# RWKV-7 triangular inverse spread over 128 partitions, with HGRN's first level by copies, fills on GpSimd and the copies into M moved ahead

## The chip, the cores and the metric

The kernel runs on one core of one Trainium2 chip. The metric is the device time of one execution, in microseconds (us). The engines are TensorE (PE, with its weight loads as PEld), VectorE (DVE), ScalarE (ACT), GpSimd (POOL) and SyncE (SP, which issues most DMAs here). Each engine runs its own instructions in order.

## The reference

One decoder layer on x of shape (1, 2048, 1024), in float32. Cut to what matters:

```
h = RMSNorm(x)
[hgrn2 columns | rwkv7 columns] = h @ W_in
HGRN2, 4 heads of 128:  S_t = diag(f_t) S_{t-1} + k_t v_t^T ;  o_t = S_t^T q_t     (k = 1 - f, chunks of 64)
RWKV-7, 8 heads of 64:  S_t = S_{t-1} diag(w_t) + (S_{t-1} a_t) b_t^T + v_t k_t^T ;  y_t = S_t r_t
x = x + concat(o_hgrn2, o_rwkv7) @ W_out
x = x + ConvFFN(RMSNorm(x))     (up-projection, causal convolution of width 3, SiLU gate, down-projection)
out = RMSNorm(x)
```

The kernel computes both recurrences by chunks. In RWKV-7 the product (S a) b^T couples the steps of a chunk, so that each chunk of 64 steps and each head needs the inverse of a unit lower triangular 64x64 matrix. In HGRN2 the decay between two steps of a chunk is a product of the f of the steps between them, and the kernel builds it in levels of a binary tree: at level l a chunk is cut into pairs of stretches of 2^l steps.

## The kernel before, in words

Phase 1 (about half of the time) makes the input projection, both mixers and the output projection of three of four blocks of 512 steps (nb = 0 to 3); phase 2 makes the last output block and the ConvFFN. A float32 product is three products of fp32r halves: each operand is split into a high half (a cast on ACT, L243 for weights, L236 for activations) and a low half (a subtraction on DVE, L244 and L237), and `mm3` issues hi x hi, hi x lo and lo x hi (L259 to L261).

**The order of the work.** Phase 1 interleaves three Python generators: `dense()` issues projections, one column job of 24 matmuls at a time (weights `wraw`, L546), and output blocks (`out_block`, activations `oraw`, L375, weights `woraw`, L382, six matmuls per k); `rw_stream` runs eight times `rw_super` (two per block); `hg_stream` runs 16 times `hg_unit` (four per block). In the loop at the end of `phase1` the two mixer generators step once each, then `fill` lets dense work go on for a credit of TICK = 2000. A list scheduler then fixes the order of each engine's instructions. A consumer waits for its producers by semaphores; a buffer with n copies comes free when its last reader is done. SP's one queue issues nearly all loads, and so weight loads stand behind whatever was put ahead of them. Only the last block's outputs are stored by GpSimd's queue (`last_dma`). Weight buffers (`wraw`, `woraw`, `oraw` share them) hold four raw tiles and four pairs of split halves.

**`rw_super`**, one half of a block (two heads pairs u, 64 triangular blocks of 32x32):
- the front makes KB, AR and the masked products M on PE (L683 to L698);
- eight DMAs take the 64 diagonal 32x32 blocks of M to DRAM (`Ed`, L711), one brings them back as E with one block on each of 64 partitions (L713);
- KBT, RHS and UV are filled by copies on ACT;
- Ti is set to the identity by two fills on DVE (L757, L758), and 31 column steps make the inverse on 64 partitions: a product E column x Ti row (L764) and an addition into the rows below (L766), with j + 1 columns and 31 - j rows at step j; a yield every four steps;
- Ti goes to DRAM (L770), a transposed copy TiT (DVE, L771) too (L772); eight DMAs bring TiT back into TTs (L779), four bring Ti back into TZ (L782);
- z (L790) and z2 (L803) combine the two diagonal 32x32 inverses of a 64x64 block with its off-diagonal block, with copies into TZ and TTs on ACT (through the helper `act`, L117);
- qus (L816) applies the inverse, one PSUM tile for each u; its result goes by seven ACT copies into M (three) and UV (four), in the order M(u0), UV, UV, M, UV, M, UV; L841 reads M, and L844, L847 (DVE) make AR; L857, L864 follow;
- the recurrence over the chunks (L875 on PE, L877 on DVE), then output and norm (L885, L893, L905) and the store to `oT` (L908). L841's tile takes the PSUM slot of the first qus tile.

**`hg_unit`**, one head of one block: k = 1 - f (L916); Sf is set to one (DVE, L927); `scaled(l)` for levels 0 to 6 makes X from q x Pf (L934) and k x Sf (L935) and updates Sf (L937) and Pf (L939); `level` multiplies X by itself on PE (L955), `take` picks the results into A (L961); two ACT copies A into Af; L990 and L991 scale k and q; L997 to L1023 finish the unit, L1029 stores to `oT`.

At level 0 a stretch has one step, Sf is still one and Pf is still f.

Of the kernel before, what the change touches and what calls it, by code (L numbers as in the profile page):

```python
# [7 lines left out]
F32 = mybir.dt.float32  # L8
# [3 lines left out]
AF = mybir.ActivationFunctionType  # L12
# [6 lines left out]
P = 128  # L19
# [42 lines left out]
def tile_layer(ctx, tc, consts, x, norm1_w, w_in, hg_lb_logits, hg_norm_w, rw_shift_mu, rw_w0, rw_w2,  # L62
# [3 lines left out]
    nc = tc.nc  # L66
    V, S, TE = nc.vector, nc.scalar, nc.tensor
    dma = nc.sync.dma_start

    cp = ctx.enter_context(tc.tile_pool(name="cp", bufs=1, reuse_waits="tile"))  # L70
    dp = ctx.enter_context(tc.tile_pool(name="dp", bufs=1, space=DRAM))
# [37 lines left out]
    def act(out_, in_, func, **kw):  # L109

        want = tables.get(func)
        if want is not None and want != tab["now"]:
            pre = S.preload_act_table_set(want)
            for u_ in tab["uses"]:
                tc.add_manual_dep(pre.ins, u_.ins.name, NOSYNC, reason="table order")
            tab.update(now=want, pre=pre, uses=[])
        i_ = S.activation(out_, in_, func, **kw)  # L117
        if want is not None:
            tc.add_manual_dep(i_.ins, tab["pre"].ins.name, NOSYNC, reason="table order")
            tab["uses"].append(i_)  # L120
        return i_
# [13 lines left out]
    with tc.tile_pool(name="vp", bufs=1, reuse_waits="tile") as vp, tc.tile_pool(name="ps0", bufs=1, space=PSUM, reuse_waits="tile") as pools["ps"]:  # L135
        rows = vp.tile([P, P], F32, name="rows")
        V.memset(rows, 0.0)
        n = 0
# [124 lines left out]
    def phase1(c1):  # L263
# [3 lines left out]
        rp = c1.enter_context(tc.tile_pool(name="rp", bufs=1, reuse_waits="tile"))  # L267
# [10 lines left out]
        TTs = hp.tile([P, 16, 64], F32, name="TTs")  # L278
# [326 lines left out]
        er0 = lambda e: 64 if e == 0 else 0  # L605

        def quads():

            return [(b, h, e, u) for b in range(4) for h in range(2) for e in range(2) for u in U]

        def col0(u, e):

            return er0(e) if u == 0 else 64 - er0(e)
# [3 lines left out]
        U = range(2)  # L617

        def rw_super(nb, s_):

            tl = stage[("tl", nb)]
            r, k, v = (stage.pop(("rkv", nb, s_, w)) for w in range(3))
# [3 lines left out]
            def tile_(tag, shape, name):  # L626
                return rp.tile([P] + shape, F32, tag=tag, name=name)

            def bank2():
                return ps.tile([P, 2, BLK], F32, tag="rw", name="rw", bufs=2)  # L630

            ai = tile_("KBT", [2, 2, BLK], "ai")
            a, iW = ai[:, 0], ai[:, 1]
# [9 lines left out]
            c, km, sq = mk_[:, 0], mk_[:, 1], mk_[:, 2]  # L643
# [43 lines left out]
            M = tile_("M", [2, 2, 4, 2, P], "M")  # L687
            for j in range(2):
                for u in U:
                    s1 = bank2()  # L690
                    for i in range(4):
                        b, e = 2 * j + i // 2, i % 2
# [9 lines left out]

            E = rp.tile([P, 32, 32], F32, tag="E", name="E")
            Ed = dp.tile([64, 32, 32], F32, tag="Ed", name="Ed", bufs=2)
            Td = dp.tile([2, 64, 32, 32], F32, tag="Td", name="Td", bufs=2)
            for u in U:
                for e in range(2):
                    for q in range(2):
                        r0 = er0(e) + 32 * q
                        m0 = u * 32 + (e * 2 + q) * 8  # L710
                        dma(Ed[m0:m0 + 8].rearrange("m s t -> s m t"),  # L711
                            M[r0:r0 + 32, u, e, :, :, 32 * q:32 * q + 32].rearrange("p b h t -> p (b h) t"))
            dma(E[0:64], Ed)  # L713

            KBT = tile_("KBT", [2, 8, P], "KBT")
            for u in U:
# [7 lines left out]
            UV = tile_("UV", [8, 2, P], "UV")  # L724
# [18 lines left out]
            for b, h, e, u in quads():  # L743
                kr, c0, sl = 64 - er0(e), col0(u, e), (b * 2 + h) * 64
# [5 lines left out]
            for e in range(2):  # L750
                r0, c0 = er0(e), col0(1, e)
                act(RHS[r0:r0 + 64, 4:8, :, 64:128], lvv[c0:c0 + 64, 1], AF.Copy)
            yield

            n = 64
            Ti = rp.tile([P, 32, 32], F32, tag="Ti", name="Ti")
            V.memset(Ti[0:n], 0.0)  # L757
            V.memset(Ti[0:n].rearrange("m a b -> m (a b)")[:, 0:1024:33], 1.0)  # L758
            yield
            for j in range(31):  # L760
                nr, ncol = 31 - j, j + 1
                tmp = rp.tile([P, 272], F32, tag="etmp", name="etmp")
                tv = tmp[0:n, 0:nr * ncol].rearrange("m (a b) -> m a b", b=ncol)
                V.tensor_mul(tv, E[0:n, j, j + 1:32].unsqueeze(2).broadcast_to([n, nr, ncol]),  # L764
                             Ti[0:n, j, 0:ncol].unsqueeze(1).broadcast_to([n, nr, ncol]))
                V.tensor_add(Ti[0:n, j + 1:32, 0:ncol], Ti[0:n, j + 1:32, 0:ncol], tv)  # L766
                if j % 4 == 3:
                    yield
            TiT = rp.tile([P, 32, 32], F32, tag="E", name="TiT")
            dma(Td[0], Ti[0:n])  # L770
            V.tensor_copy(TiT[0:n], Ti[0:n].rearrange("m a b -> m b a"))  # L771
            dma(Td[1], TiT[0:n])  # L772
            TZ = tile_("XH", [2, 2, 4, 2, 32], "TZ")
            for u in U:
                for e in range(2):
                    r0 = er0(e)
                    for q in range(2):
                        m0 = u * 32 + (e * 2 + q) * 8
                        dma(TTs[r0 + 32 * q:r0 + 32 * q + 32, 8 * u:8 * u + 8, 32 * q:32 * q + 32],  # L779
                            Td[1, m0:m0 + 8].rearrange("m s t -> s m t"))  # L780
                    m0 = u * 32 + e * 16
                    dma(TZ[r0:r0 + 32, 0, u].rearrange("p b h t -> p (b h) t"),  # L782
                        Td[0, m0:m0 + 8].rearrange("m s t -> s m t"))
            for _ in range(2):
                yield
            z = bank2()
            for b, h, e, u in quads():
                r0 = er0(e)
                c0, sl = r0 + 32 - 32 * u, u * 256 + (b * 2 + h) * 32
                TE.matmul(z[c0:c0 + 32, 0, sl:sl + 32], M[r0:r0 + 32, u, e, b, h, 32:64],  # L790
                          TZ[r0:r0 + 32, 0, u, b, h, :], start=True, stop=True, tile_position=(r0, c0))
            for u in U:
                for e in range(2):
                    r1 = er0(e) + 32
                    c0 = r1 - 32 * u
                    act(TZ[r1:r1 + 32, 1, u].rearrange("p b h t -> p (b h t)"),
                        z[c0:c0 + 32, 0, u * 256:u * 256 + 256], AF.Copy)
            yield
            z2 = bank2()
            for b, h, e, u in quads():  # L800
                r0 = er0(e)
                c0, sl = r0 + 32 * u, u * 256 + (b * 2 + h) * 32
# [3 lines left out]
            for u in U:  # L806
                for e in range(2):
                    r0 = er0(e)
                    c0 = r0 + 32 * u
# [3 lines left out]
            qus = [bank2() for _ in U]  # L813
            for b, h, e, u in quads():
                r0, c0, sl = er0(e), col0(u, e), ((b % 2) * 2 + h) * P
                TE.matmul(qus[u][c0:c0 + 64, b // 2, sl:sl + P], TTs[r0:r0 + 64, u * 8 + b * 2 + h, :],  # L816
                          RHS[r0:r0 + 64, 4 * u + b, h, :], start=True, stop=True, tile_position=(r0, c0))
            for u in U:
                quv = qus[u].rearrange("p j (b h t) -> p (j b) h t", h=2, t=P)
                bs = slice(4 * u, 4 * u + 4)  # L820
                if u == 0:
                    act(M[:, u, 0, :, :, 0:64], quv[:, :, :, 0:64], AF.Copy)
                for e in range(2):
                    r0, c0 = er0(e), col0(u, e)
                    if u == 1:
                        act(M[r0:r0 + 64, u, 0, :, :, 0:64], quv[c0:c0 + 64, :, :, 0:64], AF.Copy)
                    act(UV[r0:r0 + 64, bs, e, :].rearrange("p b (h t) -> p b h t", t=64),
                        quv[c0:c0 + 64, :, :, 64:128], AF.Copy)
            yield
            for u in U:  # L830
                Q, G = M[:, u, 0, :, :, 0:64], M[:, u, 1, :, :, 0:64]
# [21 lines left out]
            for u in U:  # L853
                for ch in range(8):
                    b, e = ch // 2, ch % 2
# [4 lines left out]
            for u in U:  # L860
                for ch in range(8):
                    b, e = ch // 2, ch % 2
# [6 lines left out]
            for ch in range(8):  # L869
                b, e = ch // 2, ch % 2  # L870
# [42 lines left out]
        def hg_unit(nb, j):  # L913
            q, f, v, gg = (stage.pop((n_, nb, j)) for n_ in "qfvg")
            k = rp.tile([P, BLK], F32, tag="hk", name="hk")
# [8 lines left out]
            A = rp.tile([P, 4, 64], F32, tag="hA", name="A")  # L924
            Pf = f
            Sf = rp.tile([P, BLK], F32, tag="Sf", name="Sf")
            V.memset(Sf, 1.0)  # L927

            def scaled(l):

                m = 1 << l
                X = rp.tile([P, BLK], F32, tag="hX", name="hX", bufs=3)
                vw = lambda t_: t_.rearrange("p (n e m) -> p n e m", e=2, m=m)
                V.tensor_mul(vw(X)[:, :, 1, :], vw(q)[:, :, 1, :], vw(Pf)[:, :, 1, :])  # L934
                V.tensor_mul(vw(X)[:, :, 0, :], vw(k)[:, :, 0, :], vw(Sf)[:, :, 0, :])  # L935
                n_ = BLK // (2 * m)
                V.tensor_mul(vw(Sf)[:, :, 0, :], vw(Sf)[:, :, 0, :],  # L937
                             vw(Pf)[:, :, 1, m - 1:m].broadcast_to([P, n_, m]))
                V.tensor_mul(vw(Pf)[:, :, 1, :], vw(Pf)[:, :, 1, :],  # L939
                             vw(Pf)[:, :, 0, m - 1:m].broadcast_to([P, n_, m]))  # L940
                return X
# [24 lines left out]
            for l in range(3):  # L966
                Xs.append(scaled(l))
                yield
# [9 lines left out]
            for l in range(3, 6):  # L978
                Xs.append(scaled(l))
                yield  # L980
# [8 lines left out]
            X = scaled(6)  # L989
# [101 lines left out]
    with ExitStack() as c2:  # L1091
# [35 lines left out]
        with tc.tile_pool(name="op", bufs=1, reuse_waits="tile") as op_:  # L1127
# [4 lines left out]
            b = NBLK - 1  # L1132
# [34 lines left out]
            for dh in range(2):  # L1167
                accs = [pst("wacc") for _ in range(4)]
                for n, k in enumerate((0, 1, 4, 5, 2, 3, 6, 7)):
# [10 lines left out]
                    if dh == 1 and 2 <= n:  # L1180
                        for j in range(2):
                            q = 2 * (n - 2) + j
# [198 lines left out]
    with tc.tile_pool(name="dn", bufs=1, reuse_waits="tile") as dn:  # L1381
# [59 lines left out]
        for s_ in range(3, N):  # L1441
            g, p, kk = steps[s_]
# [53 lines left out]
```

## Time and profile before

| what | value |
|---|---|
| time, median of three runs | 2762.55 us (2758.13 to 2766.44) |
| the profiled execution: its own time, its span | 2766.94 us, 2765.2 us |
| mean granted TensorE clock | 0.983 |
| ACT busy | 1426.2 us |
| issues of E, TZ, TTs on SP | 8, 32, 64 |

A row of the profile that begins with a line and an engine is a group of equal instructions: operation, output<-input by the program's names, partitions x elements, count | busy us in total, mean ns of one | idle time of the engine just before them, and what ended it. A row of waits reads: engine, what waited, <- what released it: us in total, times, longest. A row of the timeline begins with start and length in us, and ends with the idle time before it in brackets. "pj", "rw", "hg" and "wacc" are PSUM tiles of dense work, `rw_super`, `hg_unit` and the last output block.

### The profile page before, as it was taken

How to read it: one execution, taken by the hardware profiler on the slowest of the kernel's cores; microseconds unless marked ns; L12 is line 12 of the kernel's file. 1: busy time of each engine (PE TensorE's matmuls, PEld its weight loads, DVE VectorE, ACT ScalarE, POOL GpSimd, SP SyncE). 2: the span in 40 equal slices, each digit the busy share in tenths (PEclk: the TensorE clock that was granted, in tenths of full speed). 3: DMA queues.
4: the chain of work that ended last, by engine and by line, in shares of the span. 5: the costliest groups of instructions: out<-in, count | busy, mean ns of one | idle time of the engine just before them, and what ended most of it. 6: DMA issues, size and time to landing. Idle time of an engine off the chain costs nothing. (4 is left out here: it accounts for less than half of the span.)

```text
span 2765.2 us, 47846 instructions
## 1 busy us (share of the span) xinstructions
PE 2650.8 (96%) x18059; PEld 2107.8 (76%) x18059; DVE 2067.1 (75%) x3877; ACT 1426.2 (52%) x2304; POOL 11.1 (0%) x24
## 2 busy tenths in 40 slices
PE   8999999989999999999889999998999999999998
PEld 6877777766776777767667888786888888877887
DVE  5868787685686766768658889988997877677656
ACT  5455354644645446445346755455545555445444
POOL 0000000000000000000000000000000000000000
PEclk9999999989999899999999999999999999999999
DMA  5222322236331443633475358747662223999865
GB/s 164 77 71 67 102 77 72 69 114 188 115 112 55 111 155 123 193 105 90 144 264 170 115 191 265 230 152 228 211 227 92 88 73 132 333 331 317 287 195 185
DMA packets 429629, 435.01 MB, mean 157 GB/s; under 512 B 68704, under 2 KB 288214, under 8 KB 429398
## 3 DMA queue, kind: packets, MB, share of 16 engines
q1 hardware_dynamic: 428337, 429.30, 48.9%
q8 instruction: 142, 2.33, 0.3%
q0 software_dynamic: 992, 2.64, 0.2%
q14 instruction: 90, 0.73, 0.1%
q10 hardware_dynamic: 68, 0.02, 0.0%
HBM read 325.94 MB, written 105.91 MB: 156 GB/s over the span
## 5 line engine op out<-in xcount | busy, mean ns | idle before, releaser
L259 PE MATMUL pj<-hh,wh 128*128 128x512 f32 x960 | 401.5, 418 | 1.3 <-DVE xh L398 1.2
L260 PE MATMUL pj<-hl,wh 128*128 128x512 f32 x960 | 380.7, 397 | 0.0
L261 PE MATMUL pj<-hh,wl 128*128 128x512 f32 x960 | 379.6, 395 | 0.1
L243 ACT CAST wh<-wraw 128x512 fp32r<-128x512 f32 x240 | 147.5, 618 | 312.7 <-PE pj L260 245.4
L259 PE MATMUL ua<-Bh,uwh 128*128 128x512 f32 x704 | 279.0, 396 | 18.5 <-ACT uwh L243 14.0
L261 PE MATMUL ua<-Bh,uwl 128*128 128x512 f32 x704 | 276.4, 393 | 0.5 <-DVE uwl L244 0.5
L260 PE MATMUL ua<-Bl,uwh 128*128 128x512 f32 x704 | 276.5, 393 | 0.0
L244 DVE TENSOR_TENSOR wl<-wraw,wh 128x512 fp32r<-128x512 f32 x240 | 163.8, 686 | 119.1 <-ACT wh L243 116.3
L259 PEld LDWEIGHTS pj<-hh,wh 128*128 128x128 f32 x960 | 181.0, 189 | 53.5 <-issue 11.1
L260 PEld LDWEIGHTS pj<-hl,wh 128*128 128x128 f32 x960 | 181.2, 189 | 41.8 <-issue 7.5
L261 PEld LDWEIGHTS pj<-hh,wl 128*128 128x128 f32 x960 | 180.9, 188 | 40.0 <-DVE wl L244 1.0
L243 ACT CAST uwh<-uraw 128x512 fp32r<-128x512 f32 x220 | 134.1, 617 | 141.6 <-PE ua L260 67.6
L243 ACT CAST dah<-draw 128x512 fp32r<-128x512 f32 x151 | 93.8, 621 | 177.6 <-DMA draw<-Sg 51.2
L244 DVE TENSOR_TENSOR uwl<-uraw,uwh 128x512 fp32r<-128x512 f32 x220 | 147.0, 686 | 49.2 <-ACT uwh L243 49.0
L244 DVE TENSOR_TENSOR dal<-draw,dah 128x512 fp32r<-128x512 f32 x151 | 104.2, 690 | 100.2 <-ACT dah L243 97.7
L259 PEld LDWEIGHTS ua<-Bh,uwh 128*128 128x128 f32 x704 | 133.4, 190 | 48.8 <-ACT uwh L243 14.5
L261 PEld LDWEIGHTS ua<-Bh,uwl 128*128 128x128 f32 x704 | 133.7, 190 | 30.2 <-DVE uwl L244 2.2
L260 PEld LDWEIGHTS ua<-Bl,uwh 128*128 128x128 f32 x704 | 133.6, 190 | 27.1
L259 PE MATMUL ud<-Bh,uwh 128*128 128x512 f32 x352 | 138.0, 392 | 2.0 <-DVE cv L1347 2.0
L261 PE MATMUL ud<-Bh,uwl 128*128 128x512 f32 x352 | 137.1, 389 | 0.0
L260 PE MATMUL ud<-Bl,uwh 128*128 128x512 f32 x352 | 137.0, 389 | 0.0
L260 PE MATMUL da<-dbl,dah 128*128 128x512 f32 x340 | 133.6, 393 | 1.6 <-DVE dbl L244 1.3
(314 smaller groups left out, 5909.6 us busy)
## 6 DMA issues: line engine op xcount, KB each, us to landing
wraw<-in_w_in_dram SPq DMA_DIRECT2D x240, 256.0 KB, 3.3
uraw<-in_w_up_dram SPq DMA_DIRECT2D x176, 256.0 KB, 3.2
woraw<-in_w_out_dram SPq DMA_DIRECT2D x96, 256.0 KB, 3.1
draw<-Sg SPq DMA_DIRECT2D x88, 256.0 KB, 3.0
draw<-Tw SPq DMA_DIRECT2D x88, 256.0 KB, 4.1
gd<-y SPq DMA_DIRECT2D x86, 256.0 KB, 3.1
xt<-x1d SPq DMA_DIRECT2D x32, 512.0 KB, 6.3
draw<-gd SPq DMA_DIRECT2D x63, 256.0 KB, 4.6
```

Source lines behind the costliest of these rows:

```text
L243: S.copy(hi, src)
L244: V.tensor_sub(lo, src, hi.bitcast(F32))
L259: TE.matmul(acc, lh, rh, start=first, stop=False, skip_group_check=skip)
L260: TE.matmul(acc, lh, rl, start=False, stop=False, skip_group_check=skip)
L261: TE.matmul(acc, ll, rh, start=False, stop=last, skip_group_check=skip)
```

## The change

Four edits; none touches a matmul.

1. Inverse. Even columns of the 64 inverses lie on partitions 0 to 63, odd columns on 64 to 127. Ti is [128, 32, 16]; a step j runs over j // 2 + 1 columns. E is loaded twice, once for each half of the partitions. Ti is filled by GpSimd (one fill of 128x512, two of 64 partitions x 16). TiT is copied by ACT (128x512). Each of the 8 loads into TTs becomes two (16 partitions each, every second one), each of the 4 loads into TZ becomes two with pieces of 16 elements. The copies from z into TZ permute columns in the same way.
2. HGRN level 0: k x Sf and the update of Sf become two ACT copies (k into X, f into Sf).
3. The fill of Sf goes from DVE to GpSimd.
4. The seven copies behind qus: the three into M first, then the four into UV.

```diff
-            Td = dp.tile([2, 64, 32, 32], F32, tag="Td", name="Td", bufs=2)
+            Td = dp.tile([2, 2, 64, 512], F32, tag="Td", name="Td", bufs=2)
...
-            dma(E[0:64], Ed)
+            for f in range(2):
+                dma(E[64 * f:64 * f + 64], Ed)
...
-            n = 64
-            Ti = rp.tile([P, 32, 32], F32, tag="Ti", name="Ti")
-            V.memset(Ti[0:n], 0.0)
-            V.memset(Ti[0:n].rearrange("m a b -> m (a b)")[:, 0:1024:33], 1.0)
+            Ti = rp.tile([P, 32, 16], F32, tag="Ti", name="Ti")
+            nc.gpsimd.memset(Ti, 0.0)
+            for f in range(2):
+                nc.gpsimd.memset(Ti[64 * f:64 * f + 64].rearrange("m a b -> m (a b)")[:, 16 * f:16 * f + 496:33], 1.0)
             yield
             for j in range(31):
-                nr, ncol = 31 - j, j + 1
-                tmp = rp.tile([P, 272], F32, tag="etmp", name="etmp")
-                tv = tmp[0:n, 0:nr * ncol].rearrange("m (a b) -> m a b", b=ncol)
-                V.tensor_mul(tv, E[0:n, j, j + 1:32].unsqueeze(2).broadcast_to([n, nr, ncol]),
-                             Ti[0:n, j, 0:ncol].unsqueeze(1).broadcast_to([n, nr, ncol]))
-                V.tensor_add(Ti[0:n, j + 1:32, 0:ncol], Ti[0:n, j + 1:32, 0:ncol], tv)
+                nr, ncol = 31 - j, j // 2 + 1
+                tmp = rp.tile([P, 144], F32, tag="etmp", name="etmp")
+                tv = tmp[:, 0:nr * ncol].rearrange("m (a b) -> m a b", b=ncol)
+                V.tensor_mul(tv, E[:, j, j + 1:32].unsqueeze(2).broadcast_to([P, nr, ncol]),
+                             Ti[:, j, 0:ncol].unsqueeze(1).broadcast_to([P, nr, ncol]))
+                V.tensor_add(Ti[:, j + 1:32, 0:ncol], Ti[:, j + 1:32, 0:ncol], tv)
...
-            TiT = rp.tile([P, 32, 32], F32, tag="E", name="TiT")
-            dma(Td[0], Ti[0:n])
-            V.tensor_copy(TiT[0:n], Ti[0:n].rearrange("m a b -> m b a"))
-            dma(Td[1], TiT[0:n])
+            TiT = rp.tile([P, 16, 32], F32, tag="E", name="TiT")
+            dma(Td[0].rearrange("f m n -> (f m) n"), Ti.rearrange("m a b -> m (a b)"))
+            act(TiT, Ti.rearrange("m a b -> m b a"), AF.Copy)
+            dma(Td[1].rearrange("f m n -> (f m) n"), TiT.rearrange("m a b -> m (a b)"))
...
-                        dma(TTs[r0 + 32 * q:r0 + 32 * q + 32, 8 * u:8 * u + 8, 32 * q:32 * q + 32],
-                            Td[1, m0:m0 + 8].rearrange("m s t -> s m t"))
+                        for f in range(2):
+                            dma(TTs[r0 + 32 * q + f:r0 + 32 * q + 32:2, 8 * u:8 * u + 8, 32 * q:32 * q + 32],
+                                Td[1, f, m0:m0 + 8].rearrange("m (c t) -> c m t", t=32))
                     m0 = u * 32 + e * 16
-                    dma(TZ[r0:r0 + 32, 0, u].rearrange("p b h t -> p (b h) t"),
-                        Td[0, m0:m0 + 8].rearrange("m s t -> s m t"))
+                    for f in range(2):
+                        dma(TZ[r0:r0 + 32, 0, u].rearrange("p b h t -> p (b h) t")[:, :, 16 * f:16 * f + 16],
+                            Td[0, f, m0:m0 + 8].rearrange("m (t c) -> t m c", c=16))
...
-                    act(TZ[r1:r1 + 32, 1, u].rearrange("p b h t -> p (b h t)"),
-                        z[c0:c0 + 32, 0, u * 256:u * 256 + 256], AF.Copy)
+                    act(TZ[r1:r1 + 32, 1, u].rearrange("p b h (c f) -> p (b h) f c", f=2),
+                        z[c0:c0 + 32, 0, u * 256:u * 256 + 256].rearrange("p (s f c) -> p s f c", f=2, c=16), AF.Copy)
...
-            for u in U:
-                quv = qus[u].rearrange("p j (b h t) -> p (j b) h t", h=2, t=P)
-                bs = slice(4 * u, 4 * u + 4)
-                if u == 0:
-                    act(M[:, u, 0, :, :, 0:64], quv[:, :, :, 0:64], AF.Copy)
+            quv = [qus[u].rearrange("p j (b h t) -> p (j b) h t", h=2, t=P) for u in U]
+            act(M[:, 0, 0, :, :, 0:64], quv[0][:, :, :, 0:64], AF.Copy)
+            for e in range(2):
+                r0, c0 = er0(e), col0(1, e)
+                act(M[r0:r0 + 64, 1, 0, :, :, 0:64], quv[1][c0:c0 + 64, :, :, 0:64], AF.Copy)
+            for u in U:
                 for e in range(2):
                     r0, c0 = er0(e), col0(u, e)
-                    if u == 1:
-                        act(M[r0:r0 + 64, u, 0, :, :, 0:64], quv[c0:c0 + 64, :, :, 0:64], AF.Copy)
-                    act(UV[r0:r0 + 64, bs, e, :].rearrange("p b (h t) -> p b h t", t=64),
-                        quv[c0:c0 + 64, :, :, 64:128], AF.Copy)
+                    act(UV[r0:r0 + 64, 4 * u:4 * u + 4, e, :].rearrange("p b (h t) -> p b h t", t=64),
+                        quv[u][c0:c0 + 64, :, :, 64:128], AF.Copy)
...
-            V.memset(Sf, 1.0)
+            nc.gpsimd.memset(Sf, 1.0)
...
-                V.tensor_mul(vw(X)[:, :, 0, :], vw(k)[:, :, 0, :], vw(Sf)[:, :, 0, :])
                 n_ = BLK // (2 * m)
-                V.tensor_mul(vw(Sf)[:, :, 0, :], vw(Sf)[:, :, 0, :],
-                             vw(Pf)[:, :, 1, m - 1:m].broadcast_to([P, n_, m]))
+                if l == 0:
+                    act(vw(X)[:, :, 0, :], vw(k)[:, :, 0, :], AF.Copy)
+                    act(vw(Sf)[:, :, 0, :], vw(Pf)[:, :, 1, :], AF.Copy)
+                else:
+                    V.tensor_mul(vw(X)[:, :, 0, :], vw(k)[:, :, 0, :], vw(Sf)[:, :, 0, :])
+                    V.tensor_mul(vw(Sf)[:, :, 0, :], vw(Sf)[:, :, 0, :],
+                                 vw(Pf)[:, :, 1, m - 1:m].broadcast_to([P, n_, m]))
```

## The prediction

> **What bounds the kernel now.** I read the busy times first, then waits by engine, then single stretches.
>
> ```profile
> PE 2650.8 (96%) x18059; PEld 2107.8 (76%) x18059; DVE 2067.1 (75%) x3877; ACT 1426.2 (52%) x2304; POOL 11.1 (0%) x24
> ```
>
> TensorE (PE) is busy 96% of the 2765.2 us span. A change that leaves its instructions alone, as this one does (13,917 before and after), can only shorten the time in which PE stands still or runs at a lower granted clock. All edits lie in the mixers, which end some 1400 us into the run; the rest of PE's order is the same. The windows view gives the stock (span, length, busy us of PE, PEld, DVE, ACT, POOL, then the granted clock): first the whole of the part that the change touches, then the stretches in which the eight triangular inverses run (from the issue of E to the first store of Td; two of them and the sum), then five stretches right behind inverses 4, 6, 7 and 8.
>
> ```profile
> 0.00:1520.00 1520.00, 1433.20 (x12725) 1112.00 (x12726) 1093.55 (x2420) 779.87 (x1277) 10.00 (x22) 0.98 0.40 120
> ```
> ```profile
> 543.20:590.00 46.80, 42.55 (x362) 33.36 (x360) 41.79 (x117) 24.31 (x39) 0.00 (x0) 1.00 0.33 103
> ...
> 904.70:951.00 46.30, 43.43 (x366) 35.85 (x365) 40.32 (x114) 24.15 (x38) 0.00 (x0) 0.96 0.33 97
> ...
> sum 382.10, PE 371.76 PEld 302.74 DVE 335.48 ACT 192.55 POOL 1.12; mean PE 46.47 PEld 37.84 DVE 41.94 ACT 24.07 POOL 0.14
> ```
> ```profile
> 590.00:611.00 21.00, 13.74 (x262) 10.98 (x262) 17.21 (x47) 6.26 (x15) 0.00 (x0) 0.70 0.45 115
> 951.00:972.00 21.00, 16.96 (x252) 12.63 (x250) 14.09 (x32) 9.29 (x20) 0.00 (x0) 0.67 0.55 149
> 1170.00:1199.00 29.00, 25.39 (x304) 18.34 (x302) 20.08 (x54) 6.68 (x14) 0.00 (x0) 0.88 0.50 146
> 1323.00:1352.00 29.00, 25.25 (x363) 19.23 (x365) 17.86 (x46) 10.94 (x24) 0.00 (x0) 0.88 0.38 106
> 1352.00:1372.00 20.00, 16.50 (x303) 12.97 (x293) 10.62 (x23) 8.83 (x18) 0.54 (x1) 0.83 0.51 162
> sum 120.00, PE 97.84 PEld 74.14 DVE 79.85 ACT 42.00 POOL 0.54; mean PE 19.57 PEld 14.83 DVE 15.97 ACT 8.40 POOL 0.11
> ```
>
> Up to 1520 us PE stands still for 1520 - 1433.2 = 86.8 us: that is the whole stock. VectorE (DVE) works 335.48 of 382.10 us (88%) during the inverses, so the inverse looks like the bottleneck, but PE lacks only 382.10 - 371.76 = 10.3 us there: projections and output products fill it. More is lost just behind inverses: 120.00 - 97.84 = 22.2 us idle, and a clock of 0.67 to 0.88 that takes 0.30 x 21 + 0.33 x 21 + 0.12 x 58 + 0.17 x 20 = 23.6 us of full speed. The waits say who ends the idle time:
>
> ```profile
> PE rw L841 <- ACT UV L117: 9.8, 10, 2.1
> ...
> PE hg L997 <- DVE hk L990: 9.3, 6, 2.9
> PE wacc L259 <- ACT Bh L236: 8.6, 1, 8.6
> PE pj L259 <- ACT wh L243: 6.2, 8, 1.6
> ```
> ```profile
> ACT Af L117 <- DVE A L961: 35.3, 6, 13.6
> ...
> DVE etmp L764 <- DMA E<-Ed: 21.5, 6, 7.1
> ```
>
> No single wait holds more than 10 us of PE, and none is the inverse itself. The largest concern the copies behind L816, the end of the HGRN chain (L990), and the hand-over to the last output block.
>
> **The change part by part.** Durations are means of groups (count | busy us, mean ns).
>
> ```profile
> L937 DVE TENSOR_TENSOR Sf<-Sf,hf 128x256 f32<-128x256 f32 x112 | 47.0, 419 | 0.7
> ...
> L935 DVE TENSOR_TENSOR hX<-hk,Sf 128x256 f32<-128x256 f32 x112 | 46.8, 418 | 0.1
> ...
> L771 DVE COPY TiT<-Ti 64x1024 f32<-64x1024 f32 x8 | 8.4, 1050 | 0.1
> L927 DVE MEMSET Sf<- 128x512 f32 x16 | 7.8, 485 | 0.9
> ...
> L757 DVE MEMSET Ti<- 64x1024 f32 x8 | 7.3, 912 | 1.3 <-issue 1.1 <-PE pj L260 0.2
> ...
> L764 DVE TENSOR_TENSOR etmp<-E,Ti 64x256 f32<-64x256 f32 x8 | 3.3, 409 | 0.0
> ...
> L764 DVE TENSOR_TENSOR etmp<-E,Ti 64x31 f32<-64x31 f32 x16 | 2.9, 180 | 21.6 <-DMA E<-Ed 21.5
> ```
>
> Inverse: an instruction costs (409 - 180) / 225 = 1.02 ns per element of a partition. The elements of 31 steps are the sum of (31 - j)(j + 1) = 5456 before and of (31 - j)(j//2 + 1) = 2856 after. Two instructions a step save 2 x 2600 x 1.02 = 5.3 us of DVE per super. The Ti fills (0.91 + 0.09) and the TiT copy (1.05) leave DVE as well: 7.4 us of about 42 per inverse, 59 us for eight. Level 0 of HGRN: two products of 0.42 us in 16 units, 13.4 us; Sf fills 7.8 us. **DVE loses about 80 us.** None of it is a gain of time by itself.
>
> What comes in: on ScalarE (ACT) 32 copies of 256 elements and eight of 512; on GpSimd 24 fills of 128x512 and 16 small ones; on SyncE (SP) 104 more DMA issues: E one more per super, TZ four, TTs eight. Nearest rows:
>
> ```profile
> L117 ACT ACTIVATE UV<-rw 64x512 f32<-64x512 f32 x32 | 18.7, 586 | 0.2
> ...
> L117 ACT ACTIVATE Af<-A 64x256 f32<-64x256 f32 x32 | 13.3, 414 | 35.6 <-DVE A L961 35.3
> ```
> ```profile
> L277 POOL MEMSET Sc<- 128x512 f32 x1 | 0.5, 524 | 0.0
> ```
> ```profile
> 592.62 0.83 SPq L782 DMA_DIRECT2D TZ<-Td  x2
> 594.18 3.41 SPq L779 DMA_DIRECT2D TTs<-Td  x6
> ...
> 599.66 0.39 SPq L375 DMA_DIRECT2D oraw<-oT  x1
> ```
>
> ACT gains 32 x 0.41 + 8 x 0.59 = 18 us of an engine that is half idle; GpSimd 24 x 0.52 = 13 us. GpSimd's queue runs in order, and in the compiled order the last block's fills stand behind stores of oT of earlier units. Those units are finished before the next unit's levels begin, so I cost the fills at nothing; if that cover went, a unit of HGRN would wait for a store. A sentence of the Trainium skill speaks against fills on GpSimd: "SBUF — State Buffer", section "Who interferes with whom", says that GpSimd and DVE share a pair of ports as an exclusive lock, against DVE's two-port copies and tensor_scalar operations. By that page each fill could hold DVE for its length, 24 x 0.52 = 12.5 us of DVE at the most; no run here shows it, and the sum goes without it.
>
> The 12 loads of TZ and TTs hold SP from 592.62 to 599.66 (7.0 us), 0.41 to 0.57 us each. **24 will take 24 x 0.49 = 11.8 us**, and weight loads (the oraw at 599.66) are queued behind. The pieces of TZ halve to 64 bytes.
>
> ```profile
> TZ<-Td SPq DMA_DIRECT2D x32, 32.0 KB, 1.8
> ```
>
> In "DMA: Bandwidth & Descriptors", section "Specifications", the Trainium skill puts the smallest piece for full rate at 512 bytes. By that the 64-byte pieces would cost transfer time; the present 128-byte pieces break that rule already and land in 1.8 us, so the sum uses the issue time alone.
>
> Terms of the sum:
> 1. Inverse stretches. Idle 10.3 us, mostly in supers 4 and 6 (4.25 and 2.87), where PE waits for short DVE work that is queued between inverse steps. In the compiled order the last step of the inverse moves ahead of only one to three weight halves, so the schedule does not shrink by 7.4 us; DVE's load falls from 88% to about 72%. I take **-6**, between 0 and -10.
> 2. Stretch behind inverses 4, 6 and 8, the ones beside an output block, where dense work stops altogether. In super 4:
>
> ```profile
> 602.99 1.07 PE L790 MATMUL rw<-TZ,M 32*32 32x32 f32 x62
> 606.00 1.09 PE L997 MATMUL hg<-ident,hk 128*128 128x128 f32 x4 [1.94 <-DVE hk L990]
> ...
> 609.50 1.22 PE L259 MATMUL pj<-wh,hh 128*128 128x512 f32 x2
> ```
>
> Dense work resumes at 609.50, after HGRN's chain on DVE that ends in L990. The chain holds one Ti fill (0.91) and one level 0 (2 x 0.42): up to 1.75 us go. Against it: the block of loads starts some 2 us sooner (term 1), lasts 4.8 us longer and ends 2.8 us later, at 602.4; the last TZ lands at 602.4 + 1.8 = 604.2, where L790 starts now at 602.99, and PE's order puts L790 ahead of L997. The two nearly cancel: **-1 each, -3**, between +5 and -6 each.
> 3. The hand-over to the last block:
>
> ```profile
> 1396.14 0.39 PE L260 MATMUL pj<-wl,hh 128*128 128x512 f32 x1
> 1396.37 0.39 PE L261 MATMUL pj<-wh,hl 128*128 128x512 f32 x1
> 1405.39 0.80 PE L259 MATMUL wacc<-woh,Bh 128*128 128x512 f32 x1 [8.64 <-ACT Bh L236]
> ```
>
> PE waits 8.64 us for the store of super 8's output and its reload. In the compiled order L893 of that super comes 15 dense products earlier, 15 x 0.23 = 3.4 us, and these fill the gap: **-3.4**, between 0 and -8.6.
> 4. M copies first. L841 of u0 reuses the PSUM of the first product and starts after the last read of it: three copies now, five then, since two M copies of 64x512 move ahead (2 x 0.6). u1 still waits for the seventh. PE waits for u0 up to 1.2 us longer and gets 0.8 of it back at u1: +0.4 in each of eight supers, **+3**, between -4 and +9.
> 5. Level 0 by copies adds a wait: DVE's update of Pf (L939) must come after ACT's copy out of Pf, and ACT is often parked on a weight cast that waits for PE. Behind L939 stand the other levels and weight halves (wl), for which dense products wait. Outside the stretches of term 2 PE has other work: **+1**, between -3 and +16 (1 us a unit).
> 6. Clock: a tenth of the 23.6 us returns with a tenth less idle time: **-2**, between +6 and -10.
>
> Sum: -6 - 3 - 3.4 + 3 + 1 - 2 = -10.4. The profiled execution took 2766.94 us, 4.4 above the median of 2762.55; off the median it gives 2752, and I round to **2753 us**.
>
> **Rivals.**
> (a) Nothing comes of it: idle PE in the inverses is there for other reasons, the change in the tail is eaten by the reload. Terms 1 and 3 then fall to -2 each and the rest cancels: about 2759. For it speaks that PE is full in most inverse stretches while DVE is at 88%.
> (b) Slower, by SP: the block of 24 loads holds the output blocks' weights. Its price is 4.8 us on each of supers 4, 6 and 8, or 14, and a clock that stays low 10 us longer at 0.7, or 3; it decides once the last TZ lands later than HGRN's chain lets L997 start (606.00 in super 4 now, 604.3 without the 1.75). With terms 3 and 4 kept: +14 + 3 - 3.4 + 3 - 4 = +12, 2775. For it speaks that these blocks use up one pair of weight halves in 1.4 us (six products of 0.23), so few are in stock; against it, that today L997 waits for DVE until 6 us behind the block.
> (c) Much faster: with ACT no longer held 13.6 us on L961, the standing stretches shrink to half and the clock stays up: 11 us idle and 12 us of clock, with terms 1 and 3 about -30: 2733.
> The Trainium skill ("TensorE: Matmul & The Clock Gate", section "Part 1: The HAM clock gate") tells of a clock that falls after a spell of idleness; the 0.70 and 0.67 above agree, and by it case (c) would gain in steps.
> (d) Slower, by ACT: the copies of level 0 queue behind casts (term 5 at its upper end, +16): with the others about +6, 2768.
>
> **How the numbers follow.** My forecast, -10 with its own range 2746 to 2758, has 0.38; (a) 0.24; (b) 0.16; (c) 0.12; (d) 0.10. 0.3% is 8.3 us, about what a measurement of this kernel can tell from no change; the bound at 2754.3 cuts through my own case, of which about 0.8 lies on the faster side: 0.30 + 0.12 (c) and a little of (a) give 0.45 faster. Slower, above 2770.8: (b) and a half of (d) and some of unforeseen order, 0.25. Same: 0.30. The range reaches to (c) and (b): 2733 to 2776.
>
> **What would show it.** Right: DVE about 80 us less busy, ACT 18 more; in the windows of the inverses PE idle under 5 us; the wait of wacc L259 at 4 to 6 us; L841's wait a little up. Wrong by (b): SP's block of 24 issues of 11 us or more with a PE gap and a clock under 0.7 behind it, and woraw loads that end ACT's waits in place of L961. By (d): DVE waiting for ACT's Sf copy at L939. By (c): 590 to 611 us filled, at a clock near 1. If PE's idle time up to 1520 us stays within 5 us of 86.8, (a) holds.

## The result, and the profile after

The changed kernel takes 2781.51 us in the median of five runs (2771.89 to 2782.31), beside 2764.35 for the kernel before (five runs): a ratio of 1.0057, 95% interval 1.0043 to 1.0071, or about 16 us **slower**. The forecast was 2753, with a range up to 2776. The likeliest case was wrong, and rival (b) named what cost the time: the queue of SP.

Busy times of the changed kernel first, then its windows (span, length, busy us of PE, PEld, DVE, ACT, POOL, then the granted clock, and what the DMA engines did: busy share, GB/s). The profiled execution is the fastest of the five (2771.89 us).

```profile
PE 2646.1 (96%) x18059; PEld 2108.7 (76%) x18059; DVE 1997.4 (72%) x3805; ACT 1448.1 (52%) x2344; POOL 25.5 (1%) x64
```
```profile
0.00:1520.00 1520.00, 1421.91 (x12690) 1105.28 (x12691) 1021.43 (x2341) 797.04 (x1308) 24.44 (x62) 0.98 0.41 120
```
```profile
543.60:585.00 41.40, 40.57 (x358) 32.75 (x357) 34.90 (x115) 23.73 (x39) 0.53 (x1) 1.00 0.38 112
...
908.30:949.30 41.00, 40.55 (x363) 33.61 (x362) 34.19 (x113) 23.60 (x37) 0.53 (x1) 1.00 0.35 102
...
sum 326.50, PE 324.44 PEld 267.96 DVE 266.92 ACT 171.40 POOL 4.24; mean PE 40.55 PEld 33.49 DVE 33.36 ACT 21.43 POOL 0.53
```

The eight inverses did what was hoped. From the issue of E to the first store of Td they take 326.5 us where they took 382.1, and PE lacks 326.50 - 324.44 = 2.1 us in them where it lacked 10.3. DVE has lost 70 us. PE's matmuls are the same (18059 in both profiles; the 13,917 of the prediction stands in no view). Yet up to 1520 us PE stands still for 98.1 us, 11.3 more than before. The loss sits behind the inverses. The sums of the 50 us from the end of inverses 4, 6 and 8, first of before (from 590, 951 and 1323), then of the changed kernel (from 585, 949.3 and 1320.4), differ by 11.3 us of PE (3.0, 6.9 and 1.5):

```profile
sum 150.00, PE 129.22 PEld 99.83 DVE 90.17 ACT 54.60 POOL 0.54; mean PE 43.07 PEld 33.28 DVE 30.06 ACT 18.20 POOL 0.18
```
```profile
sum 150.00, PE 117.89 PEld 91.46 DVE 81.92 ACT 56.79 POOL 3.15; mean PE 39.30 PEld 30.49 DVE 27.31 ACT 18.93 POOL 1.05
```

Two windows behind inverses 4 and 6, the same of before and of the changed kernel:

```profile
588.00:620.00 32.00, 23.58 (x421) 18.45 (x424) 21.14 (x54) 11.84 (x25) 0.00 (x0) 0.73 0.46 129
950.00:982.00 32.00, 26.41 (x497) 20.21 (x498) 20.04 (x41) 14.58 (x29) 0.00 (x0) 0.79 0.54 155
```
```profile
588.00:620.00 32.00, 22.66 (x351) 17.97 (x352) 18.98 (x49) 9.38 (x20) 0.56 (x2) 0.73 0.31 81
950.00:982.00 32.00, 19.97 (x308) 14.34 (x311) 14.06 (x30) 13.12 (x26) 0.77 (x3) 0.73 0.42 118
```

PE is busy there for 42.6 of 64 us, where it was 50.0. The waits of PE, then those of ACT and DVE, in the changed kernel (in total, times, longest; its line numbers are a few higher: L793 is z, L843 is L841 of before, L918 makes hk):

```profile
PE pj L259 <- ACT wh L243: 12.8, 12, 2.3
PE rw L793 <- DMA TZ<-Td: 11.1, 5, 7.0
...
PE wacc L259 <- ACT Bh L236: 6.2, 1, 6.2
...
PE rw L843 <- ACT UV L117: 2.4, 3, 1.4
```
```profile
DVE etmp L765 <- DMA E<-Ed: 28.6, 6, 8.9
ACT hX L117 <- DVE hk L918: 27.7, 12, 14.1
...
DVE hk L918 <- DMA oT<-osq: 18.3, 4, 12.9
```

PE's wait for TZ was 1.7 us before, DVE's for the oT store 10.0, and DVE's for E, which is now loaded twice, 21.5. How one late queue reaches four engines shows behind inverse 6. SP, in the order of time (start, length):

```profile
950.88 0.32 SPq L785 DMA_DIRECT2D TZ<-Td  x1
951.51 2.55 SPq L781 DMA_DIRECT2D TTs<-Td  x4
...
962.12 2.49 SPq L781 DMA_DIRECT2D TTs<-Td  x4
964.65 1.08 SPq L785 DMA_DIRECT2D TZ<-Td  x2
965.83 0.40 SPq L1035 DMA_DIRECT2D oT<-osq  x1
966.32 0.38 SPq L375 DMA_DIRECT2D oraw<-oT  x1
966.79 0.41 SPq L382 DMA_DIRECT2D woraw<-in_w_out_dram  x1
```
```profile
967.97 0.43 DVE L918 TENSOR_SCALAR hk<-hf 128x512 f32<-128x512 f32 x1 [12.90 <-DMA oT<-osq]
```
```profile
968.44 0.45 ACT L117 ACTIVATE hX<-hk 128x256 f32<-128x256 f32 x1 [14.09 <-DVE hk L918]
```
```profile
963.45 0.39 PE L793 MATMUL rw<-TZ,M 32*32 32x32 f32 x4 [6.96 <-DMA TZ<-Td]
967.29 1.03 PE L793 MATMUL rw<-TZ,M 32*32 32x32 f32 x58 [3.45 <-DMA TZ<-Td]
...
972.17 1.22 PE L259 MATMUL pj<-wh,hh 128*128 128x512 f32 x2
```

The 24 loads hold SP from 950.88 to 965.73, 14.9 us. PE waits 10.4 us for TZ, whose last piece is issued at the end of the block. Behind the block stands the store of a finished HGRN unit (oT); the next unit's k needs that buffer, so DVE waits 12.9 us; the new level-0 copy on ACT needs k, so ACT waits 14.1 us, with casts of weights queued behind it. Weights and activations for dense work are on SP behind the store.

Behind inverse 4 the loss has another form. There PE has no long wait for TZ. The last 58 of z's 64 products now stand, in PE's built order, behind the end of an HGRN unit, where before they ran at 602.99, ahead of L997; z's copies (into TZ) follow on ACT, and the cast for dense work behind them:

```profile
610.54 0.70 PE L793 MATMUL rw<-TZ,M 32*32 32x32 f32 x58
...
614.73 0.73 PE L259 MATMUL pj<-wh,hh 128*128 128x512 f32 x2 [1.03 <-ACT wh L243]
```
```profile
611.32 1.62 ACT L117 ACTIVATE TZ<-rw 32x256 f32<-32x256 f32 x4
...
614.06 0.62 ACT L243 CAST wh<-woraw 128x512 fp32r<-128x512 f32 x1
```

Dense work, which stopped at 592.2 (592.9 before), resumes at 614.73 and not at 609.50. Behind inverse 8 z's last products stood at the end of an HGRN unit already before; PE's longest wait for TZ there is 0.2 us, and little is lost. So the loss shows in two ways: as a wait behind inverse 6, and as another built order behind inverse 4.

### The profile page after: what moved, and what is told of

It is laid out like the page before. It is cut to its first block, busy times and chain, and to the rows that moved or that the text cites. A ratio compares the mean times of both kernels' runs of the same rounds, so it can differ in the third digit from the quotient of the medians.

```text
span 2770.0 us, 48044 instructions
## 1 busy us (share of the span) xinstructions
PE 2646.1 (96%) x18059; PEld 2108.7 (76%) x18059; DVE 1997.4 (72%) x3805; ACT 1448.1 (52%) x2344; POOL 25.5 (1%) x64
## 4 chain that ended last, share of the span: by engine, by line
PE 75%; DVE 10%; ACT 6%; DMA 5%; issue 3%; SPq 1%; DVEq 0%; POOL 0%; ACTq 0%
PE pj L259 8%; PE pj L260 7%; PE pj L261 7%; PE ua L259 5%; PE ua L261 5%; PE ua L260 5%; PE ud L259 3%; PE ud L260 3%; PE ud L261 3%; PE da L260 2%; PE da L261 2%; PE da L259 2%; PE db L259 2%; PE db L261 2%; PE db L260 2%
## 5 line engine op out<-in xcount | busy, mean ns | idle before, releaser
L259 PEld LDWEIGHTS pj<-hh,wh 128*128 128x128 f32 x960 | 181.0, 189 | 53.9 <-issue 11.1
```

What stands on the lines that cost most here:

```text
L259: TE.matmul(acc, lh, rh, start=first, stop=False, skip_group_check=skip)
```

## The experiments

Theory A: SP is held by the longer block of loads, and z, weights and stores are late. Theory B: the copies of level 0 hold ACT, and the casts behind them. After the first four runs a rival C was added: not SP's time, but the smaller transfers. The runs were made in four groups with the kernel before beside them in each, where it took 2759.6 to 2767.1; so ratios to it are compared.

**One suspect at a time.** loads24 is the kernel before with its twelve loads split, nothing else:

```diff
-                        dma(TTs[r0 + 32 * q:r0 + 32 * q + 32, 8 * u:8 * u + 8, 32 * q:32 * q + 32],
-                            Td[1, m0:m0 + 8].rearrange("m s t -> s m t"))
+                        for f in range(2):
+                            dma(TTs[r0 + 32 * q + f:r0 + 32 * q + 32:2, 8 * u:8 * u + 8, 32 * q:32 * q + 32],
+                                Td[1, m0:m0 + 8].rearrange("m (c f) t -> f c m t", f=2)[f])
```
(and TZ in two halves of 16 columns each)

> The kernel before with nothing changed but the loads of TTs and TZ, which are split as in the changed kernel (24 issues in place of 12 per super). Theory A (the block of 24 issues holds SP about 15 us where 12 held it 6 to 7, in the trace of the changed kernel 587.1 to 603.1 in super 4): most of the loss is here, 12 to 20 us slower than before, with longer standstills of dense work behind inverses 4, 6 and 8. Theory B (copies of level 0 on ACT wait for hk and hold the weight casts behind them, 27.7 us of waits in the changed kernel): within 4 us of before.

inverse_only is the edit of the inverse with all that belongs to it; `scaled`, the fill of Sf and the order into M are those of before:

> The inverse on 128 partitions alone, with its two loads of E, GpSimd fills, TiT by ACT and 24 loads; level 0, fill of Sf and copies into M as before. Theory A: 10 to 18 us slower than before, as the changed kernel is. Theory B: no slower than before, 0 to 8 us faster.

no_inverse is the rest: level 0 by copies, fill of Sf on GpSimd, M first:

> Level 0 by copies, fill of Sf on GpSimd and copies into M first, the inverse as before. Theory A: within 6 us of before on either side. Theory B: 10 to 18 us slower than before.

loads12 keeps the whole change, but stores each half of Ti and TiT to its place in the old layout, and loads as before:

```diff
-            dma(Td[1].rearrange("f m n -> (f m) n"), TiT.rearrange("m a b -> m (a b)"))
+            for f in range(2):
+                dma(Td[1].rearrange("m (c f) t -> f m c t", f=2)[f], TiT[64 * f:64 * f + 64])
```
(the same for Td[0], and the loads of the kernel before)

> The changed kernel, but Ti and TiT are stored in two halves each, so that the layout in DRAM is that of the kernel before and TTs and TZ take 12 loads (per super 4 stores and 12 loads, in place of 2 and 24). Theory A: the loss goes, and what the shorter inverse can give is seen: 4 to 12 us faster than before, SP held 8 us or less. Theory B: as slow as the changed kernel, 10 to 18 us above before.

Measured, as ratios to the kernel before (95% interval): loads24 **1.0129** (1.0111 to 1.0147; 2803.27 us), inverse_only 1.0051 (1.0033 to 1.0069), no_inverse 0.9994 (0.9981 to 1.0007), loads12 0.9994 (0.9984 to 1.0005; 2765.84 us). Theory B falls: with the copies and no split loads nothing is lost, and with split loads alone more is lost than by the whole change, about 36 us. That was twice what theory A had expected. In the profile of loads24 PE stands still for 106.0 us up to 1520 (86.8 before), and the granted clock over the span is 0.974 (0.983 before); 0.009 x 2800 is some 25 us of full speed. Both forms of the loss are there with the inverse of before: behind inverse 4 z's last products stand behind the end of the HGRN unit, behind inverse 6 PE waits 10.8 us for TZ. So the loss of the change comes from the twelve more loads.

loads12 also missed its 4 to 12 us of gain. In its profile SP's block is down to 5.8 to 7.0 us, but PE waits for TZ seven times, 15.3 us in all. Its halves of Ti land 4.2 us after their issue (2.8 for the whole Ti in the changed kernel), and the last load of TZ stands at the end of the block behind inverse 4. That this eats the gain is not shown by a run of its own.

**SP's time or the transfers?** tts_pool is the changed kernel with one word changed, the 16 loads into TTs by `nc.gpsimd.dma_start`:

> The changed kernel, with its 16 loads into TTs per super issued by GpSimd in place of SP; TZ's 8 stay on SP, the transfers are the same. Theory A (the time that SP is held, not the transfers): SP's block falls to about 5 us, and the time comes back to that of the kernel before or below, 2755 to 2768. Rival C (the smaller and scattered transfers themselves, which TTs and TZ wait for): it stays at 2776 to 2785, and PE waits for TTs in place of TZ.

loads6_old changes the order of the 64 blocks in DRAM in the kernel before, so that one load serves both u:

```diff
-                        m0 = u * 32 + (e * 2 + q) * 8
+                        m0 = (e * 4 + q * 2 + u) * 8
...
+                    dma(TTs[r0 + 32 * q:r0 + 32 * q + 32, :, 32 * q:32 * q + 32],
+                        Td[1, m0:m0 + 16].rearrange("m s t -> s m t"))
```

> The kernel before with the 64 blocks in another order in DRAM, so that one load serves both u: 4 loads into TTs and 2 into TZ per super in place of 8 and 4, the same bytes; nothing else. Theory A: SP's block falls from 6 to 3 us, 3 to 12 us faster than before (where twelve more issues cost 36.6 us). Rival C: no change, within 3 us.

loads6_new is loads12 with the same order and six loads:

> The changed kernel with the storing in halves of loads12 and six loads per super. Theory A: faster than loads12 (2765.84) by 3 to 10 us. If the inverse on 128 partitions is worth anything in itself, it is also faster than loads6_old.

> The changed kernel once more, for a second profile, since the first was of its fastest run (2771.89, four others 2780 to 2782). Expected by theory A: the same waits and standstills as in the first profile, and if the run takes about 2781, a lower granted clock behind inverses 4, 6 or 8, 0.979 over the whole.

tts_pool: **0.9954** (0.9938 to 0.9970), 2753.86 us; the same transfers, slower each (3.5 us to landing for 2.1), and 28 us less than the changed kernel, so rival C falls for them. loads6_new: 0.9963 (0.9952 to 0.9975), some 9 us below loads12, as expected. loads6_old: 1.0005 (0.9996 to 1.0015), a miss for theory A as it stood: SP's block was 3.0 to 4.5 us long in place of 5.8 to 6.9, and that paid nothing in the kernel before.

The second profile of the changed kernel, of a run of 2784.25 us, shows the same standstills at a lower clock (0.979 over the span for 0.984; PE stands still for 100.6 us up to 1520). First profile (2771.89 us), then second:

```profile
300.00:400.00 100.00, 95.45 (x1074) 73.67 (x1073) 64.81 (x136) 49.73 (x77) 0.53 (x1) 1.00 0.31 83
600.00:700.00 100.00, 89.87 (x867) 66.08 (x866) 51.16 (x95) 44.57 (x75) 0.53 (x1) 0.94 0.54 171
1200.00:1300.00 100.00, 96.73 (x1020) 74.29 (x1018) 65.36 (x134) 54.59 (x84) 1.82 (x3) 0.97 0.33 96
```
```profile
300.00:400.00 100.00, 95.56 (x1044) 73.39 (x1044) 64.63 (x131) 47.39 (x75) 0.53 (x1) 0.95 0.28 76
600.00:700.00 100.00, 89.14 (x886) 65.02 (x887) 53.24 (x103) 43.15 (x72) 0.53 (x1) 0.91 0.54 166
1200.00:1300.00 100.00, 93.78 (x1043) 71.67 (x1043) 60.73 (x111) 54.23 (x85) 1.82 (x3) 0.93 0.37 106
```

In these three stretches alone the clock takes (0.05 + 0.03 + 0.04) x 100 = 12 us of full speed more. So the first profile shows the waits, and the median of this kernel has a dozen microseconds of clock on top of them.

**What pays once SP is free?** Four more, all with the loads into TTs on GpSimd: the kernel before, no_inverse, loads6_new, and tts_pool with level 0 on DVE again.

> The kernel before with its 8 loads into TTs per super issued by GpSimd instead of SP, nothing else. Theory A in its first form (each microsecond of SP's block is paid): 4 to 12 us faster. Theory A with a second limit (in the kernel before the chain of DVE ends later than the block, as loads6_old showed): no change, 2762 to 2769.

> Inverse as before, with level 0 by copies, fills of Sf on GpSimd, copies into M first, and its 8 loads into TTs by GpSimd: against tts_pool (2753.86) it tells what the inverse on 128 partitions is worth once SP is free. If the inverse carries the gain: 2760 to 2767. If the other parts carry it: 2750 to 2756.

> The changed kernel with stores in halves and six loads, the four into TTs by GpSimd. Theory A with a second limit: what is left of SP's block (about 1 us) no longer matters beside loads6_new (2756.01), so 2750 to 2757; below 2748 would mean that the block still cost.

> tts_pool with level 0 of HGRN on DVE again (and its fill of Sf still on GpSimd). If the two copies on ACT hold weight casts (ACT waits for hk 14.5 us in tts_pool), it is 2 to 6 us faster than tts_pool (2753.86); if the shorter chain of DVE is worth more, it is 3 to 8 us slower.

old_pool 0.9966 (0.9953 to 0.9979); no_inverse_pool 0.9969 (0.9954 to 0.9983), between its two expectations; loads6_pool 0.9986 (0.9972 to 1.0001), a miss; no_level0_pool 0.9929 (0.9900 to 0.9957), 2748.01 us. So the kernel before paid for its block too, some 9 us, and the "second limit" falls as it was put: fewer loads on SP do not pay there, another queue does. But GpSimd's queue is not free either: in loads6_pool its loads of 64 KB land 6.2 us after their issue, where SP's land after 2.3 in loads6_new, and PE waits 12.5 us for TTs in place of 2.2. The timeline shows a difference. In the kernel before, loads6_old and the changed kernel, no dense product stands between z and its successor z2 behind inverses 4 and 8; with TTs on GpSimd there are some. In tts_pool, behind inverse 4 (L806 is z2; rows of z2 and of dense work, in order of time):

```profile
596.70 0.24 PE L806 MATMUL rw<-TTs,TZ 32*32 32x32 f32 x2 [0.49 <-ACT TZ L117]
...
599.43 1.06 PE L259 MATMUL pj<-wh,hh 128*128 128x512 f32 x2
600.29 0.73 PE L260 MATMUL pj<-wl,hh 128*128 128x512 f32 x1
...
607.66 1.06 PE L806 MATMUL rw<-TTs,TZ 32*32 32x32 f32 x58
```
```profile
587.49 3.80 SPq L785 DMA_DIRECT2D TZ<-Td  x8
591.39 0.87 SPq L388 DMA_DIRECT2D xh<-in_x_dram  x2
592.36 0.38 SPq L375 DMA_DIRECT2D oraw<-oT  x1
```

TZ's eight loads leave in 3.8 us, the activations and weights follow at 592 instead of 604, and dense work resumes at 599.43 instead of 614.73. PE's order is fixed when the kernel is built, and every move of a load builds another one. loads6_new has no dense product between z and z2 behind these inverses either, and is faster than the kernel before all the same. How much of the loss and of the gains is order, and how much the time that SP is held, these runs do not tell: none keeps the order and changes the queue alone.

**z's own loads, or what stands behind them?** tz_first puts TZ's eight loads ahead of the sixteen into TTs, all on SP. inverse_pool is inverse_only, and no_m_pool is tts_pool with the copies in the old order:

> The changed kernel with TZ's 8 loads ahead of the 16 into TTs, all 24 on SP in one block: SP is held as long (about 15 us), but z (L790 of before) has its loads 10 us earlier. If the loss is z's own lateness (PE waited 11.1 us for TZ in the changed kernel): 8 to 14 us faster than the changed kernel, 2767 to 2774. If it is what stands behind the block on SP (weights, xh, oT stores): within 5 us of the changed kernel, 2777 to 2785.

> The inverse edit alone with the 16 loads into TTs by GpSimd; level 0, fill of Sf, order of copies into M as before. Beside no_level0_pool (2748.01) only the fill of Sf and the order of the M copies differ, costed at 0 and +3 us for the change: 2745 to 2752 if that holds, above 2756 if one of the two is worth something.

> tts_pool with the seven copies behind qus in the order of before. By the prediction's term for the copies (+3 us for the change) it is 3 us faster than tts_pool (2753.86), 2747 to 2754; if the order into M pays, 2756 or more.

tz_first: 1.0030 (1.0017 to 1.0043), as a ratio between the two expectations: about half of the loss goes, though the interval touches that of the changed kernel. PE's waits in its profile:

```profile
PE rw L809 <- DMA TTs<-Td: 7.1, 2, 5.0
...
PE rw L796 <- DMA TZ<-Td: 2.3, 5, 1.1
```

The wait for TZ is down from 11.1 to 2.3, and z2 now waits for TTs. So z's loads put first bring back about half of the loss, with another built order again. The other half stays undivided: it holds z2's wait for TTs and what stands behind the block, and dense work stops behind inverses 4, 6 and 8 for as long as in the changed kernel (24.9, 15.8 and 20.8 us; there 22.5, 15.9 and 19.5).

inverse_pool has the lowest ratio: **0.9917** (0.9899 to 0.9935), 2737.72 us beside 2759.61; its interval overlaps that of no_level0_pool and of no_m_pool, 0.9934 (0.9915 to 0.9954). Both came out below the times expected of them, in the group in which the kernel before was fastest too. In inverse_pool windows of the same length behind inverses 4 and 6 show PE 51.2 of 64 us busy:

```profile
588.00:620.00 32.00, 25.43 (x471) 19.05 (x471) 21.73 (x52) 13.20 (x26) 9.30 (x19) 0.84 0.50 145
942.00:974.00 32.00, 25.80 (x428) 19.03 (x432) 19.14 (x43) 14.29 (x28) 9.15 (x19) 0.73 0.52 155
```

Against old_pool (0.9966) the inverse is thus worth about 0.5%, or 13 us, with intervals apart. Beside the other edits it is worth less: tts_pool (0.9954) against no_inverse_pool (0.9969), 0.15% with intervals overlapping. Level 0 by copies, the Sf fill on GpSimd and M first, together, take back 0.9954 - 0.9917, about 0.4% or 10 us, intervals apart too, but only beside the new inverse: beside the old one they cost nothing (no_inverse_pool 0.9969, old_pool 0.9966). Which of them does it is not settled: no_level0_pool (0.9929) and no_m_pool (0.9934) overlap both ends.

## Why the prediction was wrong, point by point

- **Bound and stock of idle PE**: right. The matmuls are the same, and what changed is idle time up to the end of the mixers, and the clock.
- **DVE's saving**: 69.7 us for some 80. Steps of the inverse and products of `scaled` cost a little more than reckoned, the first row here against 180 + 95 x 1.02 = 277 ns:

```profile
L765 DVE TENSOR_TENSOR etmp<-E,Ti 128x126 f32<-128x126 f32 x24 | 7.0, 294 | 0.2
```
```profile
L117 ACT ACTIVATE TiT<-Ti 128x512 f32<-128x512 f32 x8 | 8.9, 1108 | 1.3 <-DVE Ti L767 1.3
...
L117 ACT ACTIVATE hX<-hk 128x256 f32<-128x256 f32 x16 | 7.2, 449 | 27.7 <-DVE hk L918 27.7
```

  TiT on ACT took 1.11 us, not 0.59: the row taken for it, UV, has as many elements per partition but is not a transposed copy. No run shows that the pattern is the reason.
- **Term 1** (inverse stretches, -6): idle time there fell by 8.3 us, so the sign and nearly the size held. But its side remark, that the schedule does not shrink by 7.4 us, was wrong: each became 6.95 us shorter, and the block of loads began 5.5 us sooner in super 4 (587.13 for 592.62), not 2.
- **Term 2** (stretch behind inverses 4, 6, 8, -3) is the step that failed: in the 50 us behind these three inverses PE's idle time grew by 11.3 us. The term priced the block at 24 x 0.49 = 11.8 us; it took 14.6 to 16.5 in the eight supers, since a load into every second of 32 partitions holds SP 0.62 us (2.49 for four) where one into 32 partitions in a row held it 0.47 (0.94 for two). And it let HGRN's chain on DVE cover the block. Behind inverse 4 that cover fell from 6.4 us to 0.5: the block ends at 603.08 (599.56 before) though it begins 5.5 us sooner, and HGRN's chain lets L997 (L1003 now) start 2.5 us sooner, at 603.54 (606.00). Behind inverse 6 there is no cover at all: the chain itself stands behind the block. What was queued behind the block on SP was named (weights), but not the oT store, nor that the next hk waits for that store's buffer, DVE for it, and ACT for DVE through the new copy. Nor did the term ask whether z would keep its place in PE's built order. Dense work stood still for 22.5, 15.9 and 19.5 us there (16.6, 7.4 and 14.8 before), 19 us more; PE fills a part of that with work of the mixers.
- **Term 3** (hand-over, -3.4): 8.64 became 6.18, -2.5. Right.
- **Term 4** (M first, +3): the wait of L841 fell from 9.8 to 2.4 us, which I had expected to grow a little. The runs leave its worth open (no_m_pool against tts_pool: 0.2% better without it, intervals overlapping).
- **Term 5** (level 0, +1): the copies did hold ACT, 27.7 us in total, but about half of that as the last link of SP's lateness; in tts_pool it is 14.5. Not the cause by itself (no_inverse 0.9994).
- **Term 6** (clock, -2): wrong in the median. The first profile lost nothing (0.984 over the span, 0.983 before), but four of the five runs had 0.979 or 0.980, where the runs of the kernel before beside the experiments had 0.981 to 0.987, 0.984 in the middle. At 2780 us, 0.004 is some 11 us, the larger part of the median's loss. The Trainium skill's page "TensorE: Matmul & The Clock Gate", section "Part 1: The HAM clock gate", ties the clock to idle spells; the low clock in the windows behind inverses 4 and 6 agrees (0.73 and 0.73; 0.73 and 0.79 before). The two profiles of the changed kernel show besides that nearly the same idle time can draw a different clock (300 to 400 us: PE busy 95.45 and 95.56 us, clock 1.00 and 0.95).
- **Rival (b)** had the block on SP and the condition (the last TZ lands after HGRN's chain lets L997 start). It saw the weights behind the block, but not the store, nor the built order. That its +12 lies close to the measured +16 is in part luck: it reckoned 14 us of standstill behind inverses 4, 6 and 8, where 11.3 came, and 3 of clock, where some 11 came in the median and none in the first profile. Its sum also has a last term of -4 that it does not name.
- **GpSimd's fills** were costed at nothing; the time of no_inverse bears that out for Sf, though ACT's new copy into Sf waited for the fill in seven units (9.8 us in the changed kernel). The lock of the Trainium skill's "SBUF — State Buffer", section "Who interferes with whom", left no mark that these runs can show.

## What to carry to other kernels

A faster step starts what follows it sooner, and that is worth only as much as the queue behind it allows: count every DMA that a change adds to an in-order queue, at the duration of its own shape, and list what stands behind the block, down to the buffers that stores set free. Read the built order again as well, since a longer block can move work in it. The same loads from an idle engine's queue turned +0.6% into -0.5%; but loads6_pool, whose larger loads landed later from there, lost against loads6_new. And when edits are bundled, time them apart: the inverse alone, with its loads on GpSimd, has the lowest ratio here (0.9917), and the other edits together cost part of its gain.

## What the runs showed of the hardware

The time for which SP is held by one issue differed with the pattern: 0.47 us for 32 partitions in a row (two in 0.94, kernel before), 0.62 for 16 partitions two apart, with half of the bytes (four in 2.49, changed kernel). GpSimd issued the latter loads at 0.52 us each (14 in 7.28, tts_pool), and they landed in 3.5 us in the median, where SP's landed in 2.1:

```profile
588.63 7.28 POOL L781 DMA_DIRECT2D TTs<-Td  x14 [0.23 <-issue]
```
